# Feature-major norms: means from one full-width matmul, and roots over rows as one power instruction on GpSimd

## The chip, the cores and the metric

One core of one Trainium2 chip runs the whole kernel in one launch. The metric is the device time of an execution in microseconds: 1962.84 us, the median of 3 runs (1962.72 to 1962.88).

## The reference

One layer of a hybrid decoder, for a prompt of 1024 tokens and 8 samples of 8 tokens, 1024 features each. Two gated feed-forward blocks enclose a mixing block with two head groups side by side (sliding-window attention, and a gated linear recurrence):

```python
def rms_norm(x, g):
    xf = x.astype(jnp.float32)
    y = xf * lax.rsqrt(jnp.mean(xf * xf, axis=-1, keepdims=True) + EPS)
    return (y * g.astype(jnp.float32)).astype(x.dtype)
...
x = x + 0.5 * rms_norm(swiglu(rms_norm(x, norm_ffn1_pre[l]), ffn1_w_gu[l], ffn1_w_down[l]), norm_ffn1_post[l])
h = rms_norm(x, norm_mix_pre[l])
z = h @ w_in[l] + b_in[l]
...                                  # attention -> a, recurrence -> o
a = rms_norm(a, attn_out_norm[l])
o = rms_norm(o, hg_out_norm[l]) * jax.nn.silu(hg)
x = x + rms_norm(jnp.concatenate([a, o], axis=-1) @ w_out[l], norm_mix_post[l])
x = x + 0.5 * rms_norm(swiglu(rms_norm(x, norm_ffn2_pre[l]), ffn2_w_gu[l], ffn2_w_down[l]), norm_ffn2_post[l])
```

So there are six norms over 1024 features per token, one over 512 features of the attention output, and one over 128 features per head of the recurrence output. Each needs a mean of squares and the inverse of a square root per token.

## The kernel before

**Products.** Tokens are cut into three groups: group 0 holds 256 prompt tokens and the 64 sample tokens (320 wide), groups 1 and 2 hold 384 prompt tokens each. A large product is made of three passes over operands that are split into a rounded high part and a low rest (`mm3`, L244 to L248: high x high, high x low, low x high). A weight tile arrives by DMA in `raw` (3 buffers), ACT casts the high part and DVE subtracts for the low part (`split`, L225 to L227), both into slots of the pool `wsp` (8). Products accumulate in four PSUM banks `mm`; four more, `ax`, serve transposes, scores and the norms. SBUF scratch tiles of up to 512 columns come from the pool `t2` (8 buffers).

**Order of the work.** The first feed-forward block runs group 0 alone at first (`pre_first`, `up0`), then all groups; the mixing block runs group by group, with the mixer of a group (`attn_block`, `intra`, `hgrn_block`) as a generator that advances between the large products (`tick`, `stream`); the second feed-forward block closes. Norm work of a group is also such a generator. The final order on every engine is made by a scheduler that goes by a model of the time; some instructions are bound to come after others (`tc.issue_after`).

**Two layouts of a norm.** Where features lie on partitions (feature-major, tokens along the free axis), squares are summed over the eight chunks of features into `ss` [128, w], and the sum over partitions must come from PE. `bcast_steps` (L276) does it for the first norm of groups 1 and 2 (`pre_x`) and for the norms of group 0 (`post_t`, `pre_t`); `pre_first` (L556) does it with `roots` (L639) for the first norm of all. The steps are: a 32-bit product of each 128-token piece of `ss` with a column `omean` of 1/1024 (`st`, L297 or L643), which puts means on partitions; the root on a [128, 3] tile; three diagonal matrices (`dg`, L305 or L650); and a product of `ones` with them (`rb`, L309 or L663), which spreads each token's root over all partitions. `rb` stays in its PSUM bank until the scaling is done (`pre_first` copies it to SBUF, L664). That happens eight times in an execution.

Where tokens lie on partitions (rows), ACT sums squares along the free axis and the root is on a tile of 1, 3 or 4 columns: `row_rms` (L369), `post_n` (L399), `finish_attn` (L1186), `finish_hgrn` (L1358) and `each` (L1739), 30 roots in all. `each` runs once per 128 rows of the last result: behind the last large product of its rows it adds (L1016), squares, takes the root, scales and adds the residual (L1742), and stores.

**The root.** `rsqrt` (L201 to L218) is a bit trick and two polynomial steps on DVE, eight instructions over several columns and six over one. ACT and POOL have no part in it.

Of the kernel before, what the change touches and what calls it, by code (L numbers as in the profile page):

```python
# [8 lines left out]
F32 = mybir.dt.float32  # L9
# [9 lines left out]
P = 128  # L19
# [26 lines left out]
def tile_step(ctx: ExitStack, tc: tile.TileContext, A: dict, O: list):  # L46
# [67 lines left out]
                pass  # L114


    ident = cp.tile([P, P], F32, name="ident")
    make_identity(nc, ident)
    ones = cp.tile([P, P], F32, name="ones")
    V.memset(ones, 1.0)  # L120
    junk = cp.tile([P, 512], BF16, name="junk")
    omean = cp.tile([P, 1], F32, name="omean")
    V.memset(omean, 1.0 / D)
    S.activation(junk[:, :P], ones, AF.Silu)
    cols = cp.tile([P, NROWS], F32, name="cols")
# [75 lines left out]
    def rsqrt(y, x, wk):  # L201
# [15 lines left out]
        V.scalar_tensor_tensor(q, t, -40.0 / 3 * RS ** 6, t, op0=ALU.add, op1=ALU.mult)  # L217
        V.scalar_tensor_tensor(y, q, 80.0 * RS ** 12, y, op0=ALU.add, op1=ALU.mult)  # L218

    def small():  # L220
        return pp.tile([P, 4, 8], F32, tag="small", bufs=10, name=uid("sm"))

# [50 lines left out]
    def tmp2(name, shape=(P, 512)):  # L273
        return pp.tile(list(shape), F32, tag="t2", bufs=8, name=uid(name))

    def bcast_steps(part, w, out, add=None):  # L276

        ss = tmp2("ss")
        for d in range(KC):
            if d == 0:  # L280
                S.activation(ss[:, :w], part(d), AF.Square)
                continue
            sq = tmp2("sq")
            S.activation(sq[:, :w], part(d), AF.Square)
            (G if add else V).tensor_tensor(ss[:, :w], ss[:, :w], sq[:, :w], op=ALU.add)
            if d % 3 == 0 or add:
                yield
        yield
        nb = (w + P - 1) // P
        bank = axbank("st")  # L290
        sm = small()
        full = w // P
        if w % P:
            V.memset(sm[:, 0, 0:nb], 1.0)
        for c in range(nb):
            n = min(P, w - c * P)
            PE.matmul(bank[:n, c:c + 1], ss[:, c * P:c * P + n], omean, start=True, stop=True)  # L297
        V.tensor_scalar(sm[:, 0, 0:full], bank[:, 0:full], EPS, None, op0=ALU.add)
        if w % P:
            V.tensor_scalar(sm[:w % P, 0, full:nb], bank[:w % P, full:nb], EPS, None, op0=ALU.add)  # L300
        rsqrt(sm[:, 1, 0:nb], sm[:, 0, 0:nb], (sm[:, 2, 0:nb], sm[:, 3, 0:nb]))
        dg = tmp2("dg")
        for c in range(nb):
            n = min(P, w - c * P)
            V.tensor_scalar(dg[:, c * P:c * P + n], ident[:, :n], sm[:, 1, c:c + 1], None, op0=ALU.mult)  # L305
        yield
        yield
        rb = axbank("rb")
        PE.matmul(rb[:, :w], ones, dg[:, :w], start=True, stop=True)  # L309
        out.append(rb)  # L310
        yield

    def post_t(y, xsrc, gpost, xdst=None):

        w = WIDTH[0]

        def part(d):
            return y[d // 4][:, d % 4, :w]

        rb = []  # L320
        yield from bcast_steps(part, w, rb)
        for d in range(KC):
            xt = tmp2("xt")
            nc.sync.dma_start(xt[:, :w], xsrc(d))
            V.scalar_tensor_tensor(part(d), part(d), gpost[:, d:d + 1], rb[0][:, :w],
                                   op0=ALU.mult, op1=ALU.mult)
            G.tensor_tensor(part(d), part(d), xt[:, :w], op=ALU.add)
            if d % 2:
                yield
        if xdst is not None:  # L330
            for hf in range(2):
                nc.sync.dma_start(xdst[:, 4 * hf:4 * hf + 4], y[hf][:, :, :w])

    def pre_t(y, gpre, h):
        w = WIDTH[0]

        def part(d):
            return y[d // 4][:, d % 4, :w]

        rb = []  # L340
        yield from bcast_steps(part, w, rb)
        h[0] = new_h(0)
        for d in range(KC):
            t = tmp2("ht")
            V.scalar_tensor_tensor(t[:, :w], part(d), gpre[:, d:d + 1], rb[0][:, :w],
                                   op0=ALU.mult, op1=ALU.mult)
            hi, lo = hcol(h[0], d, w)
            split(hi, lo, t[:, :w], G)
            if d % 2:
                yield  # L350


    def row_rms(n, y, blocks, sm, dst=None):

        b0, b1 = blocks[0], blocks[-1] + 1
        if rows_of(n, b1 - 1) < P:
            V.memset(sm[:, 0, :], 1.0)
        for i in blocks:
# [10 lines left out]
        rsqrt(sm[:, 1, b0:b1], sm[:, 0, b0:b1], (sm[:, 2, b0:b1], sm[:, 3, b0:b1]))  # L369

    def gain_row(ap, scale, hf):
        g = tmp2("gb")
# [17 lines left out]
    def post_n(n, y, sm, xsrc, xdst=None):  # L390
# [8 lines left out]
        rsqrt(sm[:, 1, 0:3], sm[:, 0, 0:3], (sm[:, 2, 0:3], sm[:, 3, 0:3]))  # L399
        for i in range(3):  # L400
            if i:
                xt = load(i)
# [49 lines left out]
    def pre_x(n, y, gpre, part, SF):  # L452
# [5 lines left out]
        yield from bcast_steps(x_part, 384, rb, True)  # L458
        part[n] = y
        for d in range(KC):  # L460
            V.scalar_tensor_tensor(x_part(d), x_part(d), gpre[:, d:d + 1], rb[0][:, :384], op0=ALU.mult, op1=ALU.mult)
# [94 lines left out]
    def pre_first(x, gpre, h, raws, wts):  # L556
# [1 line left out]


        w = WIDTH[0]  # L560
        sm = small()
# [15 lines left out]

        def x_part(d):
            return x[d // 4][:, d % 4]

        V.memset(sm[:, 0, :], 1.0)

        def half(n, k, e="V"):
            raw, (hi, lo) = raws[n], tiles[n]
# [48 lines left out]
            wts.fill(2)  # L633
        second = [mmbank(), mmbank()]
        rb = tmp2("rb")[:, :w]
        dg = tmp2("dg")
        st = axbank("st")

        def roots():  # L639
            with after("PE"):  # L640
                for i in range(3):
                    r = rows_of(0, i)
                    order("PE", PE.matmul(st[:r, i:i + 1], ss[:, i * P:i * P + r], omean, start=True, stop=True))  # L643
            with after("V"):
                V.tensor_scalar(sm[:, 0, 0:2], st[:, 0:2], EPS, None, op0=ALU.add)
                V.tensor_scalar(sm[:NS, 0, 2:3], st[:NS, 2:3], EPS, None, op0=ALU.add)
                rsqrt(sm[:, 1, 0:3], sm[:, 0, 0:3], (sm[:, 2, 0:3], sm[:, 3, 0:3]))
                for i in range(3):
                    r = rows_of(0, i)
                    order("V", V.tensor_scalar(dg[:, i * P:i * P + r], ident[:, :r], sm[:, 1, i:i + 1], None,  # L650
                                               op0=ALU.mult))

        for n, bank in enumerate(second):
            wt = wts.ready.pop(0)
            for d in range(KC):
                if n == 0 and d == 4:
                    roots()
                    with after("V"):
                        wts.fill()
                if n == 1 and d == 4:  # L660
                    with after("PE"):
# [422 lines left out]
    def mixing(tp, h):  # L1084
# [96 lines left out]
        def finish_attn(n, o, r, sl):  # L1181
# [169 lines left out]
        def finish_hgrn(n, bank, r, c0):  # L1351
# [6 lines left out]
            rsqrt(sm[:r, 1, :4], sm[:r, 0, :4], (sm[:r, 2, :4], sm[:r, 3, :4]))  # L1358
# [372 lines left out]
    def each(i):  # L1731
        need("half")
        y, sm = f2.ys[2], small()
        x, t = sm[:, 0, 1:2], sm[:, 0, 2:3]
# [3 lines left out]
        V.tensor_scalar(x, sm[:, 0, 0:1], 1.0 / D, tail["sm"][:, 1, i:i + 1], op0=ALU.mult, op1=ALU.add)  # L1738
        rsqrt(sm[:, 1, 0:1], x, (t, sm[:, 0, 3:4]))  # L1739
        t0 = 384 + i * P  # L1740
        for hf, src in ((0, yg), (1, y[1][:, i])):
            V.scalar_tensor_tensor(src, src, sm[:, 1, 0:1], tail["x"][hf][:, i], op0=ALU.mult, op1=ALU.add)  # L1742
# [87 lines left out]
```

## Time and profile before

| | |
|---|---|
| time, median of 3 runs | 1962.84 us |
| the profiled execution | 1962.94 us, span 1960.9 us |
| TensorE clock granted, mean | 0.999 |
| feature-major norms in an execution | 8 |
| `st` products (L297, L643), passes on PE | 42 + 6 |
| `rb` products (L309, L663), passes on PE | 14 + 2 |
| roots by `rsqrt` (instructions on L213) | 38 |
| instructions on DVE, on POOL | 2519, 161 |

PE is TensorE, DVE is VectorE, ACT is ScalarE, POOL is GpSimd and SP is SyncE; PEld is TensorE loading weights beside its products. A row of a group of instructions names line, engine, operation and tile (out<-in), then its count, its busy time and the mean of one in ns, then the idle time of the engine just before it and what ended that. A row of the timeline gives start, duration, engine, line and tile; in brackets stands the idle time just before it. A 32-bit product is recorded as two passes (x2). Times are us from the start of the span unless ns is said.

### The profile page before, as it was taken

The numbers are of one execution on the slowest core, as the hardware profiler recorded it, in microseconds if no ns is written. First come the engines' busy times: TensorE is split into PE (matmuls) and PEld (weight loads), VectorE is DVE, ScalarE is ACT, GpSimd is POOL, SyncE is SP. The second block draws the span as 40 slices with busy tenths as digits, with TensorE's granted clock in tenths as the row PEclk, the third lists the DMA queues.
The fourth block names the chain that finished last, engine by engine and source line by source line (L and its number), as shares of the span: only waits on it lengthen the run. The fifth ranks groups of instructions, "written<-read, shape, count | busy, mean of one in ns | idle before, by whom it ended". The sixth has DMA issues, their size and how long they took to land.

```text
span 1960.9 us, 33822 instructions
## 1 busy us (share of the span) xinstructions
PE 1946.4 (99%) x13119; PEld 1821.5 (93%) x13119; DVE 1413.4 (72%) x2519; ACT 942.5 (48%) x1694; POOL 168.3 (9%) x161
## 2 busy tenths in 40 slices
PE   9999999999999999999999999999999999999998
PEld 8999999999998988778999898989999999999886
DVE  7696769886558756777677757755987877655667
ACT  5553434444445444435345545765544444444452
POOL 0400000000004102011121203000000000000201
PEclk9999999999999999999999999999999999999999
DMA  7634547555676547764434344536555645677874
GB/s 242 205 118 169 209 166 250 198 185 194 230 240 222 178 143 238 269 199 154 117 99 151 97 136 130 163 125 222 169 201 194 215 172 187 213 233 239 302 256 141
DMA packets 174161, 371.04 MB, mean 189 GB/s; under 512 B 15968, under 2 KB 66848, under 8 KB 173984
## 3 DMA queue, kind: packets, MB, share of 16 engines
q1 hardware_dynamic: 168096, 358.06, 54.8%
q10 hardware_dynamic: 5904, 10.82, 1.6%
q8 instruction: 103, 1.69, 0.3%
q14 instruction: 58, 0.48, 0.1%
HBM read 286.41 MB, written 83.39 MB: 189 GB/s over the span
## 4 chain that ended last, share of the span: by engine, by line
PE 98%; DVE 1%; ACT 0%; DMA 0%; POOL 0%; issue 0%; SPq 0%; DVEq 0%; ACTq 0%; POOLq 0%
PE mm L246 29%; PE mm L247 29%; PE mm L248 29%; PE sc L1216 1%; PE c L248 1%; PE c L246 1%; PE c L247 1%; PE pv L1255 1%; PE lv L1302 1%; PE pT L1244 1%; PE av L1389 0%; PE u L1396 0%; PE av L1392 0%; DMA big<-in_ffn_w_gu_dram 0%; PE su L1512 0%; PE tr L435 0%
## 5 line engine op out<-in xcount | busy, mean ns | idle before, releaser
L246 PE MATMUL mm<-h,wsph 128*128 128x320 f32 (+1 forms) x1296 | 412.7, 320 | 0.0
L247 PE MATMUL mm<-h,wsph 128*128 128x320 f32 (+1 forms) x1296 | 410.9, 317 | 0.0
L248 PE MATMUL mm<-h,wspl 128*128 128x320 f32 (+1 forms) x1296 | 408.4, 316 | 0.6 <-DVE wspl L227 0.6
L227 DVE TENSOR_TENSOR wspl<-raw,wsph 128x1024 fp32r<-128x1024 f32 x204 | 252.6, 1239 | 140.1 <-ACT wsph L226 135.9
L226 ACT CAST wsph<-raw 128x1024 fp32r<-128x1024 f32 x204 | 213.6, 1049 | 289.9 <-PE mm L247 229.1
L226 ACT CAST w<-raw 128x512 fp32r<-128x512 f32 (+1 forms) x212 | 156.9, 744 | 205.5 <-PE mm L247 105.3
L246 PEld LDWEIGHTS mm<-h,wsph 128*128 128x128 f32 x1296 | 243.1, 188 | 8.6 <-issue 7.1
L247 PEld LDWEIGHTS mm<-h,wsph 128*128 128x128 f32 x1296 | 243.5, 188 | 4.4 <-issue 3.4
L248 PEld LDWEIGHTS mm<-h,wspl 128*128 128x128 f32 x1296 | 243.0, 188 | 1.9 <-DVE wspl L227 0.9
L246 PE MATMUL mm<-h,w 128*128 128x384 f32 (+1 forms) x720 | 240.5, 334 | 1.1 <-ACT h L596 1.1
L247 PE MATMUL mm<-h,w 128*128 128x384 f32 (+1 forms) x720 | 240.6, 334 | 0.2 <-DVE h L598 0.2
L227 DVE TENSOR_TENSOR w<-raw,w 128x512 fp32r<-128x512 f32 (+1 forms) x212 | 179.7, 851 | 83.4 <-ACT w L226 83.0
L248 PE MATMUL mm<-h,w 128*128 128x384 f32 (+1 forms) x720 | 235.2, 334 | 0.4 <-POOL w L589 0.4
L247 PE MATMUL mm<-w,h 128*128 128x512 f32 x462 | 181.1, 392 | 0.0
L248 PE MATMUL mm<-w,h 128*128 128x512 f32 x462 | 180.3, 392 | 0.0
L246 PE MATMUL mm<-w,h 128*128 128x512 f32 x462 | 179.4, 392 | 0.0
L247 PE MATMUL mm<-big,w 128*128 128x384 f32 x528 | 176.5, 334 | 0.0
L246 PE MATMUL mm<-big,w 128*128 128x384 f32 x528 | 176.4, 334 | 0.0
L248 PE MATMUL mm<-big,w 128*128 128x384 f32 x528 | 176.1, 334 | 0.0
L246 PEld LDWEIGHTS mm<-h,w 128*128 128x128 f32 x720 | 135.2, 188 | 1.4 <-ACT h L596 1.3
L247 PEld LDWEIGHTS mm<-h,w 128*128 128x128 f32 x720 | 135.2, 188 | 0.4 <-DVE h L598 0.4
L248 PEld LDWEIGHTS mm<-h,w 128*128 128x128 f32 x720 | 134.7, 188 | 0.7 <-POOL w L589 0.7
(346 smaller groups left out, 3454.9 us busy)
## 6 DMA issues: line engine op xcount, KB each, us to landing
raw<-in_ffn_w_gu_dram SPq DMA_DIRECT2D x158, 512.0 KB
raw<-in_ffn_w_down_dram SPq DMA_DIRECT2D x74, 512.0 KB
raw<-in_w_in_dram SPq DMA_DIRECT2D x54, 512.0 KB
ar<-fa SPq DMA_DIRECT2D x70, 384.0 KB
big<-in_ffn_w_down_dram SPq DMA_DIRECT2D x88, 256.0 KB
fb<-big SPq DMA_DIRECT2D x44, 512.0 KB
fa<-big SPq DMA_DIRECT2D x22, 768.0 KB
raw<-fb SPq DMA_DIRECT2D x30, 512.0 KB
```

What stands on the lines that cost most here:

```text
L226: made['S'] = S.copy(hi, src).ins
L227: (lo_eng or V).tensor_tensor(lo, src, hi.bitcast(F32), op=ALU.subtract)
L246: PE.matmul(out, a[0], b[0], start=first, stop=False, skip_group_check=resume)
L247: PE.matmul(out, a[0], b[1], start=False, stop=False, skip_group_check=resume)
L248: return PE.matmul(out, a[1], b[0], start=False, stop=last, skip_group_check=resume).ins
L1216: PE.matmul(banks[g][:, i * 256:i * 256 + wk], zq[64 * g:64 * g + 64, 2 * pr + i, b * P:(b + 1) * P], kx[64 * g:64 * g + 64, k0:k0 + wk], ...
L1244: PE.transpose(bank[:, (kb * 2 + i) * P:(kb * 2 + i + 1) * P], pt[g][:, i, kb * P:(kb + 1) * P], ident)
L1255: PE.matmul(ob[64 * g:64 * g + 64, pr * 256:pr * 256 + 256], vn[:, vb, 64 * g:64 * g + 64], pT[g][:, kb * 256:kb * 256 + 256], start=kb == ...
L1302: PE.matmul(b5[32 * i:32 * i + 32, b, a], K[:, a, cs], Q[:, a, cs], start=True, stop=True)
```

## The change

Feature-major: `omean` becomes a [128, 128] matrix of 1/1024, so that one 32-bit product of it with `ss` leaves every token's mean on all partitions. The root is then taken by `rsqrt` over the whole width in SBUF, and its result `rb` is used from there. The three `st` products, the diagonals and the product of `ones` with them go, as does the copy in `pre_first`. In `pre_first`, product and root are issued where `roots` stood, and no later instruction is bound to come after the last step of the root.

Rows: `root` is one power instruction on POOL with a constant tile of -0.5 as second operand, in all five places.

```diff
+    mhalf = cp.tile([P, 8], F32, name="mhalf")
+    V.memset(mhalf, -0.5)
-    omean = cp.tile([P, 1], F32, name="omean")
+    omean = cp.tile([P, P], F32, name="omean")
     V.memset(omean, 1.0 / D)
...
+    def root(y, x):
+        G.tensor_tensor(y, x, mhalf[:y.shape[0], :y.shape[-1]], op=ALU.pow)
...
+    def mean_root(rb, ss, order=None):
+        w = rb.shape[-1]
+        bank = axbank("rb")
+        PE_ = PE.matmul(bank[:, :w], omean, ss, start=True, stop=True)
+        x, t = tmp2("mx")[:, :w], tmp2("mt")[:, :w]
+        V.tensor_scalar(x, bank[:, :w], EPS, None, op0=ALU.add)
+        rsqrt(rb, x, (t, x))
+        return PE_
...
     def bcast_steps(part, w, out, add=None):
...
-        for c in range(nb):
-            n = min(P, w - c * P)
-            PE.matmul(bank[:n, c:c + 1], ss[:, c * P:c * P + n], omean, start=True, stop=True)
...
-        rsqrt(sm[:, 1, 0:nb], sm[:, 0, 0:nb], (sm[:, 2, 0:nb], sm[:, 3, 0:nb]))
-        dg = tmp2("dg")
-        for c in range(nb):
-            n = min(P, w - c * P)
-            V.tensor_scalar(dg[:, c * P:c * P + n], ident[:, :n], sm[:, 1, c:c + 1], None, op0=ALU.mult)
+        rb = tmp2("rb")[:, :w]
+        mean_root(rb, ss[:, :w])
         yield
         yield
-        rb = axbank("rb")
-        PE.matmul(rb[:, :w], ones, dg[:, :w], start=True, stop=True)
         out.append(rb)
...
     # pre_first
                 if n == 0 and d == 4:
-                    roots()
-                    with after("V"):
-                        wts.fill()
-                if n == 1 and d == 4:
-                    with after("PE"):
-                        rbank = axbank("rb")
-                        order("PE", PE.matmul(rbank[:, :w], ones, dg[:, :w], start=True, stop=True))
-                    S.copy(rb, rbank[:, :w])
+                    with after("PE"), after("V"):
+                        order("PE", mean_root(rb, ss[:, :w]))
+                    wts.fill()
...
     # finish_attn; in row_rms, post_n, finish_hgrn and each in the same way
-            rsqrt(sm[:r, 1, 0:1], sm[:r, 0, 0:1], (sm[:r, 2, 0:1], sm[:r, 3, 0:1]))
+            root(sm[:r, 1, 0:1], sm[:r, 0, 0:1])
```

More of the change, by code (lines that the diff above doesn't have):

```diff
@@ L288, in bcast_steps @@
         yield
[L289 to L294, printed above, removed]
-        for c in range(nb):
-            n = min(P, w - c * P)
[L297 to L300, printed above, removed]
-        rsqrt(sm[:, 1, 0:nb], sm[:, 0, 0:nb], (sm[:, 2, 0:nb], sm[:, 3, 0:nb]))
-        dg = tmp2("dg")
-        for c in range(nb):
-            n = min(P, w - c * P)
-            V.tensor_scalar(dg[:, c * P:c * P + n], ident[:, :n], sm[:, 1, c:c + 1], None, op0=ALU.mult)
+        rb = tmp2("rb")[:, :w]
+        mean_root(rb, ss[:, :w])
         yield
         yield
-        rb = axbank("rb")
-        PE.matmul(rb[:, :w], ones, dg[:, :w], start=True, stop=True)
         out.append(rb)
@@ L324, in post_t @@
             nc.sync.dma_start(xt[:, :w], xsrc(d))
-            V.scalar_tensor_tensor(part(d), part(d), gpost[:, d:d + 1], rb[0][:, :w],
+            V.scalar_tensor_tensor(part(d), part(d), gpost[:, d:d + 1], rb[0],
                                    op0=ALU.mult, op1=ALU.mult)
@@ L344, in pre_t @@
             t = tmp2("ht")
-            V.scalar_tensor_tensor(t[:, :w], part(d), gpre[:, d:d + 1], rb[0][:, :w],
+            V.scalar_tensor_tensor(t[:, :w], part(d), gpre[:, d:d + 1], rb[0],
                                    op0=ALU.mult, op1=ALU.mult)
@@ L368, in row_rms @@
                                op0=ALU.add, op1=ALU.add)
-        rsqrt(sm[:, 1, b0:b1], sm[:, 0, b0:b1], (sm[:, 2, b0:b1], sm[:, 3, b0:b1]))
+        root(sm[:, 1, b0:b1], sm[:, 0, b0:b1])
     def gain_row(ap, scale, hf):
@@ L398, in post_n @@
         V.scalar_tensor_tensor(sm[:, 0, 0:3], sm[:, 0, 0:3], EPS, sm[:, 0, 4:7], op0=ALU.add, op1=ALU.add)
-        rsqrt(sm[:, 1, 0:3], sm[:, 0, 0:3], (sm[:, 2, 0:3], sm[:, 3, 0:3]))
+        root(sm[:, 1, 0:3], sm[:, 0, 0:3])
         for i in range(3):
@@ L460, in pre_x @@
         for d in range(KC):
-            V.scalar_tensor_tensor(x_part(d), x_part(d), gpre[:, d:d + 1], rb[0][:, :384], op0=ALU.mult, op1=ALU.mult)
+            V.scalar_tensor_tensor(x_part(d), x_part(d), gpre[:, d:d + 1], rb[0], op0=ALU.mult, op1=ALU.mult)
             if d % 2:
@@ L560, in pre_first @@
         w = WIDTH[0]
-        sm = small()
         spare = axbank()
@@ L579, in x_part @@
             return x[d // 4][:, d % 4]
-        V.memset(sm[:, 0, :], 1.0)
         def half(n, k, e="V"):
@@ L635, in pre_first @@
         rb = tmp2("rb")[:, :w]
-        dg = tmp2("dg")
-        st = axbank("st")
-        def roots():
-            with after("PE"):
-                for i in range(3):
-                    r = rows_of(0, i)
-                    order("PE", PE.matmul(st[:r, i:i + 1], ss[:, i * P:i * P + r], omean, start=True, stop=True))
-            with after("V"):
[L645 to L651, printed above, removed]
         for n, bank in enumerate(second):
@@ L656, in pre_first @@
                 if n == 0 and d == 4:
-                    roots()
-                    with after("V"):
-                        wts.fill()
-                if n == 1 and d == 4:
-                    with after("PE"):
-                        rbank = axbank("rb")
-                        order("PE", PE.matmul(rbank[:, :w], ones, dg[:, :w], start=True, stop=True))
-                    S.copy(rb, rbank[:, :w])
+                    with after("PE"), after("V"):
+                        order("PE", mean_root(rb, ss[:, :w]))
+                    wts.fill()
                 with after("PE"):
@@ L1357, in finish_hgrn @@
             V.tensor_scalar(sm[:r, 0, :4], sm[:r, 0, :4], 1.0 / P, EPS, op0=ALU.mult, op1=ALU.add)
-            rsqrt(sm[:r, 1, :4], sm[:r, 0, :4], (sm[:r, 2, :4], sm[:r, 3, :4]))
+            root(sm[:r, 1, :4], sm[:r, 0, :4])
             V.tensor_tensor(o[:r], b4[:r], sm[:r, 1, :4].unsqueeze(2).to_broadcast([r, 4, P]), op=ALU.mult)
@@ L1733, in each @@
         y, sm = f2.ys[2], small()
-        x, t = sm[:, 0, 1:2], sm[:, 0, 2:3]
+        x = sm[:, 0, 1:2]
         S.activation(junk, y[0][:, i], AF.Square, accum_out=sm[:, 0, 0:1])
@@ L1738, in each @@
         V.tensor_scalar(x, sm[:, 0, 0:1], 1.0 / D, tail["sm"][:, 1, i:i + 1], op0=ALU.mult, op1=ALU.add)
-        rsqrt(sm[:, 1, 0:1], x, (t, sm[:, 0, 3:4]))
+        root(sm[:, 1, 0:1], x)
         t0 = 384 + i * P
```

## Prediction

> **What bounds the kernel now.** I read the busy times first, then the stages, then who waits for whom. The page of the kernel before, its first part and the shares of its chain:
>
> ```profile
> PE 1946.4 (99%) x13119; PEld 1821.5 (93%) x13119; DVE 1413.4 (72%) x2519; ACT 942.5 (48%) x1694; POOL 168.3 (9%) x161
> PE 98%; DVE 1%; ACT 0%; DMA 0%; POOL 0%; issue 0%; SPq 0%; DVEq 0%; ACTq 0%; POOLq 0%
> ```
>
> The reader sees one engine carrying everything: TensorE (PE) is busy for 1946.4 of 1960.9 us, and the chain that ended last is PE for 98%. A busy PE need not be PE at its best, so the stages matter (stretch, length, then PE, PEld, DVE, ACT and POOL busy):
>
> ```profile
> 10.00:20.00 10.00, 8.89 (x60) 8.34 (x59) 9.53 (x23) 7.85 (x16) 1.48 (x1) 1.00 0.75 280
> 60.00:100.00 40.00, 38.97 (x265) 38.17 (x264) 30.69 (x60) 20.99 (x33) 12.61 (x9) 1.00 0.52 169
> 960.00:1330.00 370.00, 367.83 (x3468) 332.17 (x3467) 260.16 (x559) 200.96 (x413) 56.09 (x48) 1.00 0.41 129
> 1950.00:1961.00 11.00, 3.46 (x16) 2.52 (x14) 6.93 (x21) 0.97 (x4) 0.00 (x0) 0.84 0.26 100
> ```
>
> The other stretches that I asked for between 20 and 1950 us are full to the hundredth. So PE idles at the start, about 1 us in 60 to 100, 2.2 us in the mixing stage, and 7.5 us after its last matmul. Three waits of PE on other engines touch the change:
>
> ```profile
> PE av L1392 <- DVE big L1341: 1.4, 1, 1.4
> PE st L297 <- POOL ss L285: 1.0, 1, 1.0
> PE st L643 <- DVE ss L625: 0.5, 1, 0.5
> ```
>
> Two kinds of edit count, then: those that change PE's own stream, and those in the last 7.5 us. Everything else on DVE or POOL is hidden as long as PE keeps its supply.
>
> **Part 1, the means: PE loses 24 matmuls.** Each of eight feature-major norms now runs three products of the summed squares with a column (`st`), a root on a [128, 3] tile, three diagonals `dg`, and a product of `ones` with them (`rb`). The change keeps one product of the shape of `rb` and drops `st`. Three of the eight places, first, second and last, in the order of time (start, us, engine, line):
>
> ```profile
> 18.57 0.81 PE L643 MATMUL st<-omean,ss 128*128 128x1 f32 x6 [0.48 <-DVE ss L625]
> 19.31 0.42 PE L246 MATMUL mm<-h,wsph 128*128 128x320 f32 x1
> 19.57 0.31 PE L247 MATMUL mm<-h,wsph 128*128 128x320 f32 x1
> ...
> 62.48 0.31 PE L248 MATMUL mm<-h,wspl 128*128 128x320 f32 x1
> 62.63 0.72 PE L297 MATMUL st<-omean,ss 128*128 128x1 f32 x6
> 63.22 0.39 PE L246 MATMUL mm<-h,wsph 128*128 128x320 f32 x1
> 63.45 0.31 PE L247 MATMUL mm<-h,wsph 128*128 128x320 f32 x1
> ...
> 1802.81 0.39 PE L248 MATMUL mm<-w,h 128*128 128x512 f32 x1
> 1803.04 0.70 PE L297 MATMUL st<-omean,ss 128*128 128x1 f32 x6
> 1803.67 0.50 PE L246 MATMUL mm<-w,h 128*128 128x512 f32 x1
> 1804.01 0.39 PE L247 MATMUL mm<-w,h 128*128 128x512 f32 x1
> ```
>
> The price of a group is read from starts: from its own start to that of the second matmul behind it, less one ordinary step. At 62.63 it is 63.45 - 62.63 - 0.15 = 0.67 us (62.63 - 62.48 is the ordinary step); at 1803.04 it is 0.97 - 0.23 = 0.74; at 18.57 it is 1.00 - 0.15 = 0.85. The other five lie between 0.64 and 0.77 by the same reading. Sum of eight: **-5.9 us**, all on the engine that is the chain.
>
> The product that stays costs what it cost:
>
> ```profile
> 585.67 0.70 PE L309 MATMUL rb<-dg,ones 128*128 128x320 f32 x2
> 585.97 0.64 PE L247 MATMUL mm<-w,h 128*128 128x512 f32 x1
> 586.45 0.40 PE L248 MATMUL mm<-w,h 128*128 128x512 f32 x1
> ```
>
> From 585.67 to 586.45 less a step is 0.55 us. Its operands change places (`omean` is stationary, `ss` moves) but the sizes are the same, so I cost the exchange at nothing. It now stands where `st` stood and takes over that wait for `ss`.
>
> Against this: the built order of the changed kernel has 313 changes between the 32-bit products and the split ones on PE, against 315 before, although dropping eight groups should take away 12 to 16. So five to seven small groups more stand alone among the large products. The row at 1803.67 shows what a return costs: 0.34 us to the next start and not 0.23, so 0.11. I add **+0.6 us** (0 to +0.8).
>
> **Part 2, the wide root on DVE.** A root over [128, 320 or 384] is nine passes over the width, in place of the small ones and the diagonals. The rows of the first norm now, and of a pass of that width:
>
> ```profile
> 19.57 0.15 DVE L645 TENSOR_SCALAR sm<-st 128x2 f32<-128x2 f32 x1
> 22.02 2.35 DVE L227 TENSOR_TENSOR wspl<-raw,wsph 128x1024 fp32r<-128x1024 f32 x2
> 25.83 0.48 DVE L742 TENSOR_TENSOR sg<-mm,rb 128x320 f32<-128x320 f32 x1
> 26.23 0.48 DVE L744 TENSOR_TENSOR su<-mm,rb 128x320 f32<-128x320 f32 x1
> ```
>
> and the cast to the high half that goes ahead of a weight subtraction (count, busy, mean ns):
>
> ```profile
> L226 ACT CAST wsph<-raw 128x1024 fp32r<-128x1024 f32 x204 | 213.6, 1049 | 289.9 <-PE mm L247 229.1
> ```
>
> Now the chain is 22.02 - 19.57 = 2.45 us; nine passes at 0.40 (26.23 - 25.83) are 3.6. DVE thus gains about 1.2 us of work in each of eight norms, some 9 us in all, and loses far more in part 3. Hidden from 60 us on, since DVE is 72% busy and PE never waits for these roots today. At the start DVE is full, so there I followed the order of the built program: the nine passes stand among weight subtractions (1.18 us each) that used to come later, and the last subtraction ahead of the first user of `rb` needs a weight slot that PE has still to free. From 19.1 us PE has half a unit of 24 matmuls left and then whole ones at 24 x 0.147 = 3.5 us: 20.9, 24.4, 27.9, 31.5. The slot comes free at 27.9, cast (1.05) and subtraction end at about 30.2, and the first user starts there, against 25.83 now. PE wants the bank that it frees at 31.5, and the parts of `h` behind it with margins of 0.2 to 1.2 us by the same count. I take **+0.3 us** (0 to +1.0). `rb` now holds an SBUF buffer of eight instead of a PSUM bank of four through the scaling; the order already contains that.
>
> **Part 3, 30 roots over rows on POOL.** Each drops six to eight DVE instructions and adds a trip to POOL and back. Only the last of them is on the path, behind PE's last matmul:
>
> ```profile
> 1953.49 0.69 DVE L1016 TENSOR_TENSOR big<-mm,big 128x512 f32<-128x512 f32 x1 [0.27 <-PE mm L248]
> ...
> 1955.03 0.21 DVE L1738 TENSOR_SCALAR sm<-sm,sm 128x1 f32<-128x1 f32 x1
> 1955.28 0.15 DVE L213 TENSOR_SCALAR sm<-sm 128x1 int32<-128x1 int32 x1
> ...
> 1956.37 0.16 DVE L218 SCALAR_TENSOR_TENSOR sm<-sm 128x1 f32<-128x1 f32 x1
> 1956.56 0.75 DVE L1742 SCALAR_TENSOR_TENSOR yg<-yg,sm,big 128x512 f32<-128x512 f32 x1
> ```
>
> That is 1956.56 - 1955.28 = 1.28 us gone. No power operation is in this trace; the nearest small ones on POOL are these:
>
> ```profile
> L1288 POOL TENSOR_TENSOR big<-big 128x8 f32<-128x8 f32 x1 | 0.2, 201 | 0.1
> L1288 POOL TENSOR_TENSOR big<-big 128x64 f32<-128x64 f32 x1 | 1.4, 1355 | 0.1
> ```
>
> Bounds: 0.2 us from below, and 1.4 from above, a row far above its neighbours. I take 0.5 for the power, since it is nearest to the 8-wide product and more work, and 0.3 for the two hops: **-0.5 us** (-0.9 to +0.4). POOL is empty from 1950 us on, so nothing is queued ahead.
>
> The other 29 lie beside PE. In the built order, DVE's reader stands directly behind its writer for 12 of the 30, so DVE is held there for the whole trip, about 0.8 us where it used to work about 1.28. POOL's long multiplications of the same layer end before the first root of the layer's blocks is due, so I expect no queue. What is behind a held DVE is the next weight subtraction; its cover is the lead that this row shows, in which DVE idles for ACT:
>
> ```profile
> 1239.56 1.22 DVE L227 TENSOR_TENSOR wspl<-raw,wsph 128x1024 fp32r<-128x1024 f32 x1 [3.14 <-ACT wsph L226]
> ```
>
> I cost these at nothing (-2 to +2 us: today's PE waits gone, or as many new).
>
> **The sum.** -5.9 + 0.6 + 0.3 - 0.5 = -5.5 us against the profiled execution's 1962.94: 1957.4. The median of the runs is 0.10 lower: **1957.3 us**.
>
> **Rivals.**
> - *New waits on DVE and POOL eat the gain* (0.14). For it: the order of the whole mixing stage is shuffled, and the margins at the start are below 1 us. Against: a held DVE comes out ahead of today's 1.28 us. With all ends at their worst, 0.8 + 1.0 + 0.4 + 2 - 5.9 = -1.7: about 1961.
> - *A slow power* (0.08), the slower side. [...] If one root takes r us, the tail pays about twice (r - 1.1), since the second block's chain ends only just ahead of 1953.49, and each of the 12 holds pays what exceeds 1.1 + 3.1. Gain and bound together are 5.5 + 3.9 = 9.4; it decides from r of about 4.4 us, and at r = 5 gives 2 x 3.9 + 12 x 0.8 - 5.0 = +12: 1975. Against: no small row of POOL is over 1.4 us.
> - *One long first root* (0.06), if POOL has to fetch the power's code. One POOL instruction of this trace did last far beyond its kind (min/median/max ns):
>
> ```profile
> L285 POOL TENSOR_TENSOR ss<-ss,sq x14: 1012/1019/5107, 51.9 to 75.7; 128x384 f32<-128x384 f32 x14
> ```
>
>   A first root of 5.1 us plus 0.3 for the hops, less a lead of 3.1, brings 2.3 us to PE in the mixing stage: about 1959.6. Against: POOL's first product of two tensors took no longer than its second.
>
> ```profile
> 7.98 1.28 POOL L589 TENSOR_TENSOR w<-big,w 128x512 fp32r<-128x512 f32 x1 [5.68 <-ACT w L587]
> 11.28 1.48 POOL L589 TENSOR_TENSOR w<-big,w 128x512 fp32r<-128x512 f32 x1 [2.02 <-ACT w L587]
> ```
>
>   [...]
> - *The 24 matmuls are no gain* (0.06): PE only waits elsewhere for the weights' DMA, and the time stays near 1962.5. Against: PE has no DMA wait from 20 us on.
>
> **How the numbers follow.** Forecast 0.66, all of it below 1958.9, which is 0.2% (3.9 us) under the median and about what a measurement of this kernel can tell from no change. The first, third and fourth rivals end within 0.2%: 0.26. The slow power is slower: 0.08. The range goes from -8.8, the best ends of all parts (-5.9 - 0.9 - 2), to -1.7, the worst ones: 1954.0 to 1961.2; outside lie the slow power, the fourth rival and little else.
>
> **What would show it.** PE's matmuls fall by 48 passes (13119 counts two of each) and its busy time by some 6 us. L297 and L643 are gone, and one two-pass group stands at each of eight places. From the last row pass of the tail to the first product with the residual: under 1.28 us. POOL gains 30 short instructions; their length decides between forecast and slow power. PE waits naming POOL `sm` or DVE in the mixing stage, over 2 us in sum, would make the prediction wrong; so would a wait for `h` between 31 and 46 us.

## The result, and the profile after

The changed kernel takes **1969.14 us**, the median of 8 runs (1966.31 to 1970.13), against 1962.87 of before in the same series (1962.72 to 1963.33): a ratio of 1.003, with a 95% interval of 1.0021 to 1.004. It is slower by 6.3 us; 5.5 us faster was forecast. The profiled execution took 1968.62 us with a span of 1966.9.

The page of the kernel after, busy times and the shares of the chain:

```profile
PE 1948.6 (99%) x13071; PEld 1817.6 (92%) x13071; DVE 1409.2 (72%) x2268; ACT 940.9 (48%) x1693; POOL 203.6 (10%) x191
...
PE 91%; DVE 2%; DMA 1%; issue 1%; ACT 1%; SPq 0%; DVEq 0%; POOLq 0%; POOL 0%; ACTq 0%
```

The 48 passes on PE are gone (13119 to 13071), DVE has 251 instructions fewer and POOL 30 more, as the edit says. But PE's busy time rose by 2.2 us where 6 less was forecast, and the chain is PE for 91% only: other engines now hold PE up. Stretches of the kernel after (length, then PE, PEld, DVE, ACT, POOL busy):

```profile
60.00:100.00 40.00, 39.05 (x261) 38.25 (x261) 37.45 (x49) 22.08 (x33) 13.13 (x9) 1.00 0.61 204
960.00:1330.00 370.00, 366.53 (x3434) 327.96 (x3433) 248.73 (x447) 197.46 (x411) 71.81 (x62) 1.00 0.40 126
```

Between 60 and 100 us DVE went from 30.69 to 37.45 us, though it has fewer instructions there (49 for 60): they got longer. PE's waits in the kernel after (us in total, times, longest):

```profile
PE mm L252 <- DVE w L232: 2.3, 2, 1.4
PE av L1364 <- DVE big L1313: 1.4, 1, 1.4
PE pT L1216 <- ACT t L1205: 1.3, 2, 1.2
...
PE mm L251 <- DVE big L993: 0.7, 1, 0.7
...
PE mm L252 <- DVE h L232: 0.7, 1, 0.7
```

All but the second are new, and none names POOL `sm`, the wait that I had feared most. The sign that I had set for a wrong prediction, new waits of PE for DVE or POOL `sm` in the mixing stage, did not show: there the only wait of PE for DVE is the old one of 1.4 us.

**Where the time went.** Both kernels run the same 10242 split products. By their names and shapes in the traces, some 390 stand at another place in the order after the change, all of them between 20 and 50, 110 and 160, 590 and 630, and 840 and 870 us; the others keep their place, and nearly the same holds for the experiments. So the start of the n-th one in each kernel shows how far it is ahead (-) or behind, in us against before:

| at (us of before) | after | rows alone | means alone, root in PSUM | whole change, both repairs |
|---|---|---|---|---|
| 30 | -1.40 | -0.52 | -1.42 | -0.95 |
| 60 | -0.01 | -0.52 | -0.67 | 0.09 |
| 100 | -1.42 | -0.54 | -2.06 | -2.53 |
| 560 | -1.22 | -0.54 | -2.06 | -2.52 |
| 700 | 0.91 | -0.54 | -3.58 | -4.04 |
| 1200 | -1.25 | -1.78 | 0.06 | -6.38 |
| 1330 | 6.27 | 5.76 | 0.05 | -7.82 |
| 1790 | 6.29 | 5.75 | 0.04 | -7.80 |
| 1850 to the end | 6.66 | 5.75 | -0.72 | -8.56 |

(The last three columns are experiments, below.) Two things must be kept in mind. Each column starts with a lead of 0.5 to 0.66 us that it has from the first 10 us, before any product of the change runs: in the kernel before, PE's first large product waited 1.1 us for ACT and started later than in the others. And the row at 1200 us catches a moment: in the kernel after, two groups of small products, 1.9 us in all, stand four split products later, while at 1190 and 1230 us its column reads 0.7. So the column of after has three places of loss: 1.4 us in 30 to 60, 2.1 in 560 to 700, and 5.5 in 1230 to 1330. The first and second lie beside feature-major norms, the third in the mixing stage, where roots over rows stand. Behind the last product the new kernel gains 0.6 us.

**The second place, read from the trace.** DVE of the kernel after from 583 us on, and PE's product that waits for it:

```profile
583.94 7.53 DVE L322 SCALAR_TENSOR_TENSOR big<-big,halfpost,rb 128x320 f32<-128x320 f32 x8
591.38 1.89 DVE L232 TENSOR_TENSOR w<-raw,w 128x1024 fp32r<-128x1024 f32 x1
```

```profile
593.32 0.50 PE L252 MATMUL mm<-w,h 128*128 128x512 f32 x1 [1.43 <-DVE w L232]
```

Eight scalings take 7.53 us, the weight subtraction behind them ends at 593.27, and PE has stood since 591.9. POOL's additions run beside them:

```profile
584.63 9.38 POOL L324 TENSOR_TENSOR big<-big,xt 128x320 f32<-128x320 f32 x8 [357.80 <-DMA xt<-in_x0T_dram]
```

Here are the same scalings by their line, before and then after (min/median/max ns):

```profile
L325 DVE SCALAR_TENSOR_TENSOR big<-big,halfpost,rb x16: 542/543/548, 586.4 to 1816.2; 128x320 f32<-128x320 f32 x16
```

```profile
L322 DVE SCALAR_TENSOR_TENSOR big<-big,halfpost,rb x16: 539/1160/1169, 583.9 to 1823.7; 128x320 f32<-128x320 f32 x16
L322 DVE SCALAR_TENSOR_TENSOR big<-big,cols,rb x8: 546/547/548, 1030.5 to 1033.8; 128x320 f32<-128x320 f32 x8
```

Same shape, same count, 543 ns then 1160. What changed is where `rb` lies: a PSUM bank before, SBUF now. And the second row of after is the same instruction at 547 ns, from 1030.5 to 1034.3 us, where POOL's additions (L324) start only at 1034.6. **Theory A**: with both tensors in SBUF the scaling and POOL's addition beside it slow each other, and the weights queued behind reach PE late. **Theory B**: the rest is the roots over rows, whose trip to POOL holds DVE and so the mixing stage. The **rival** to both is that neither matters by itself: the scheduler wrote another order for PE's small products.

### The profile page after: what moved, and what is told of

Read it like the earlier page. It is cut to its first block, busy times and chain, and to the rows that moved or that the text cites. A ratio compares the mean times of both kernels' runs of the same rounds, so it can differ in the third digit from the quotient of the medians.

```text
span 1966.9 us, 33517 instructions
## 1 busy us (share of the span) xinstructions
PE 1948.6 (99%) x13071; PEld 1817.6 (92%) x13071; DVE 1409.2 (72%) x2268; ACT 940.9 (48%) x1693; POOL 203.6 (10%) x191
## 4 chain that ended last, share of the span: by engine, by line
PE 91%; DVE 2%; DMA 1%; issue 1%; ACT 1%; SPq 0%; DVEq 0%; POOLq 0%; POOL 0%; ACTq 0%
PE mm L251 27%; PE mm L252 27%; PE mm L253 27%; DMA ar<-fa 1%; PE sc L1188 1%; PE pv L1227 1%; PE c L253 1%; PE c L251 1%; PE c L252 1%; PE pT L1216 1%; PE lv L1274 1%; DVE big L322 1%; PE av L1361 0%; DVE w L232 0%; PE u L1368 0%
## 5 line engine op out<-in xcount | busy, mean ns | idle before, releaser
L232 DVE TENSOR_TENSOR wspl<-raw,wsph 128x1024 fp32r<-128x1024 f32 x204 | 257.3, 1263 | 134.0 <-ACT wsph L231 132.5
```

The source lines that it names most:

```text
L232: (lo_eng or V).tensor_tensor(lo, src, hi.bitcast(F32), op=ALU.subtract)
```

## The experiments

Each was timed in five rounds beside the kernel before, which took 1962.68 to 1962.72 us in these series.

**1. Four kernels that take the change apart.** The means alone:

```diff
     # the changed kernel, in all five places
-            root(sm[:r, 1, 0:1], sm[:r, 0, 0:1])
+            rsqrt(sm[:r, 1, 0:1], sm[:r, 0, 0:1], (sm[:r, 2, 0:1], sm[:r, 3, 0:1]))
```

> Only the feature-major part: the means by one product, the wide root on DVE, rb in an SBUF buffer; every root over rows stays the Newton chain on DVE. Theory A (two SBUF inputs of the scalings run beside POOL's additions and slow each other; PE waits about 4.6 us for the weights queued behind them) and theory B (the roots over rows on POOL cost some 6.7 us net in the mixing stage) together: -5.9 +0.6 +4.6 +0.9 (start) = about 1963.1, the scalings with halfpost at about 1.16 us each. Rival to both (all of the loss is from the roots over rows): about 1957.5, the scalings harmless to PE.

The roots over rows alone (the five calls of `root` put into the kernel before):

> Only the roots over rows as one power on POOL; the means, diagonals and the PSUM bank of rb as before the change. Theory B: +7.3 us of PE's waits and single groups between 860 and 1330 us, less 0.6 in the tail: about 1969.5. If theory A carries the whole loss: about 1962.3.

The whole change with `rb` in PSUM again, and the means alone with it (the very first norm, in `pre_first`, keeps its root in SBUF in both):

```diff
-    def rsqrt(y, x, wk):
+    def rsqrt(y, x, wk, out=None):
...
-        V.scalar_tensor_tensor(y, q, 80.0 * RS ** 12, y, op0=ALU.add, op1=ALU.mult)
+        V.scalar_tensor_tensor(y if out is None else out, q, 80.0 * RS ** 12, y, op0=ALU.add, op1=ALU.mult)
...
-        rsqrt(rb, x, (t, x))
+        rsqrt(rb, x, (t, x), bank[:, :w] if psum else None)
...
     # bcast_steps
-        rb = tmp2("rb")[:, :w]
-        mean_root(rb, ss[:, :w])
+        rb = mean_root(tmp2("my")[:, :w], ss[:, :w], True)
```

> The changed kernel with the last step of the wide root written into the PSUM bank of the mean, so that the scalings again have one SBUF input and one PSUM input. Theory A: the scalings with halfpost go back from 1.16 to 0.54 us beside the same POOL additions, PE's waits at 591, 617, 642 and 1825 us go, about 4.6 us less than the changed kernel: 1964.5. Rival (the slow scalings are hidden, or POOL alone slows them): 1969, and 1.16 us stays if POOL alone does it.

> Only the feature-major part, with the root written into the PSUM bank; the roots over rows on DVE. Theories A and B together: -5.9 +0.6 +0.9 = about 1958.5, the fastest of the four. If the loss comes from the new order of PE's work and not from A or B: within 1 us of the kernel with the means alone.

| | us | ratio to before, 95% |
|---|---|---|
| means alone | 1965.67 | 1.0012 (1.0003 to 1.0021) |
| rows alone | 1968.22 | 1.0026 (1.0015 to 1.0036) |
| whole change, root in PSUM | 1965.32 | 1.0013 (1.0004 to 1.0022) |
| means alone, root in PSUM | 1961.92 | 0.9999 (0.999 to 1.0008) |

**Theory A holds.** The medians put the bank at 3.8 us in both pairs (1969.14 to 1965.32, 1965.67 to 1961.92). The times of the last kernel scatter widely (1959.98 to 1967.71), and its interval overlaps that of the means alone, so the second pair is weak by itself. The traces are not: between 560 and 700 us after and the means alone lose 2.1 and 1.5 us against before, and both kernels with the bank gain 1.5. The scalings of the whole change with the root in PSUM, beside the same additions on POOL:

```profile
L321 DVE SCALAR_TENSOR_TENSOR big<-big,halfpost,rb x16: 542/542/548, 583.4 to 1818.5; 128x320 f32<-128x320 f32 x16
584.05 9.27 POOL L323 TENSOR_TENSOR big<-big,xt 128x320 f32<-128x320 f32 x8 [357.80 <-DMA xt<-in_x0T_dram]
```

POOL's additions differ as well, if less clearly: the median of all 24 is 1123 ns in the kernel after and 882 here, while the eight from 584 us on take 9.38 and 9.27 us in sum.

The medians of the scaling side by side: 1160 ns with both tensors in SBUF and additions beside (kernel after), 547 with both in SBUF and no addition beside (kernel after, the row with `cols`), 542 with `rb` in PSUM and additions beside.

Theory B's number came near (1969.5 expected, 1968.22 measured). But the means alone came 2.6 us above the 1963.1 expected, and the last kernel missed by 3.4 us, with no root on POOL in it at all: it lost 3.6 us between 700 and 1200 where the two norms in that stretch should have won 1.5. Of the 5 us, 1.6 belong to the profiled execution, in which PE's granted clock (third column from the end) fell for a moment:

```profile
840.00:850.00 10.00, 10.00 (x63) 8.76 (x62) 8.57 (x17) 4.79 (x11) 0.60 (x1) 0.86 0.74 234
```

The other 3.5 strike a mixing stage that has no root on POOL.

**A third theory.** The longer steps of PE at 1245 us, where "rows alone" and after lose 1.6 us at once, lead to it. PE's small products there in the kernel before:

```profile
1245.79 1.08 PE L1255 MATMUL pv<-t,vn 128*64 128x256 f32 x8
1246.80 1.13 PE L1216 MATMUL sc<-kx,big 64*128 64x256 f32 x8
1247.87 0.49 PE L1389 MATMUL av<-big,big 128*128 128x128 f32 x2
```

and in the kernel after:

```profile
1243.75 0.65 PE L1227 MATMUL pv<-t,vn 128*64 128x256 f32 x2
1244.33 1.13 PE L1188 MATMUL sc<-kx,big 64*128 64x256 f32 x4
1245.38 1.08 PE L1227 MATMUL pv<-t,vn 128*64 128x256 f32 x6
1246.39 1.13 PE L1188 MATMUL sc<-kx,big 64*128 64x256 f32 x4
1247.45 0.49 PE L1361 MATMUL av<-big,big 128*128 128x128 f32 x2
```

The reader sees the same 8 + 8 passes take 2.08 us before and 3.70 after. Eight scores in one go cost 1.07 us (1246.80 to 1247.87), and four cost 1.06. The shapes and the starts say why: `sc` uses 64 rows of the array and `pv` 64 columns, one half for each of two heads, and the program gives the heads in turn. Standing next to each other two heads run side by side: in a whole group the trace has the passes start in pairs, 6 to 7 ns apart. Where the scheduler puts something between them, each half runs alone: the four scores at 1244.33 start one by one, 215 ns and more apart.

**Theory C**: the loss in the mixing stage is split pairs. PE's time for `sc`, and then for `pv`, in the whole execution (first column after the length), of before:

```profile
0.00:1970.00 1970.00, 21.36 (x128) 12.91 (x128) 22.45 (x64) 1.00 0.57 188
0.00:1970.00 1970.00, 19.04 (x120) 7.90 (x120) 4.68 (x8) 1.00 0.57 188
```

of after, and "rows alone" has the same two PE values:

```profile
0.00:1970.00 1970.00, 23.86 (x128) 14.12 (x128) 22.53 (x64) 1.00 0.56 188
0.00:1970.00 1970.00, 21.59 (x120) 8.61 (x120) 4.70 (x8) 1.00 0.56 188
```

40.40 us became 45.45. (These busy times count the overlap of a product's end with the next one. Counted from start to next start, as the expectations below do, it is 38.4 and 42.9: 4.55 us more.) The scheduler's order has 12 whole groups of scores and 10 of `pv` before, 9 and 6 after. The means alone with the root in PSUM fit too: with no root on POOL that kernel has 10 and 9 whole groups and 42.86 us of busy time, 2.5 more than before, of the 3.5 that were left open.

**2. Pairs bound together.** In `attn_block` each of these products is bound to come after the one ahead of it, heads in turn, the second head first because its operand is ready later:

```diff
-                    for g in range(2):
-                        PE.matmul(banks[g][:, i * 256:i * 256 + wk], ...
+                    for g in (1, 0):
+                        with tc.issue_after(prev) if prev else nullcontext():
+                            prev = PE.matmul(banks[g][:, i * 256:i * 256 + wk], ...).ins
...                  # and the same for the products into ob
```

> The kernel before the change, with the products of each attention block bound to follow one another on PE (two heads alternate, the second head first, the four scores behind the four value products): theory C says that two heads' half-array products run side by side when they stand next to each other, so that a whole group costs 1.0 us and a split one 1.6 to 2.1. Scores and value products together now take 38.4 us; with 13 whole groups of each and 3 split ones some 34.8: 3.5 us less, about 1959.3. Rival (the pairs do not matter, the mixing stage waits on DVE, ACT or POOL): 1962.7, unchanged.

> The roots over rows on POOL as the only part of the change, with the attention products bound in the same way. Theory C: the loss of this part is the split pairs, 42.9 us of scores and value products against 34.8 when bound, so 1968.2 - 8.1 = about 1960, within 1 us of the bound kernel before. Theory B (the loss is the trip to POOL and back with DVE held behind it): the two bound kernels still differ by about 5.5 us, 1965 here.

> The whole change with the attention products bound. Theory C: 1969.1 - 8.1 = about 1961; what is left above the forecast is theory A's 3.7 us. Theory B: about 1967.

> The version that the theories point to: means by one product with the root written into the PSUM bank, the power on POOL only for the last rows (each), every other root over rows on DVE, attention products bound. From the kernel with the means and the bank: -5.3 for the pairs, -0.6 for the tail: 1961.9 - 5.9 = about 1956. If pairs do not matter: 1961.3.

| | us | `sc` + `pv` us, unbound to bound | ratio to before, 95% |
|---|---|---|---|
| before, bound | 1960.13 | 40.40 to 37.14 | 0.9989 (0.998 to 0.9998) |
| rows alone, bound | 1958.29 | 45.45 to 36.50 | 0.9975 (0.9965 to 0.9985) |
| whole change, bound | 1959.04 | 45.45 to 36.50 | 0.9979 (0.997 to 0.9988) |
| means in PSUM, power in the tail, bound | 1956.59 | (no unbound twin) 37.83 | 0.9973 (0.9964 to 0.9983) |

The place shown above, in "rows alone, bound":

```profile
1241.69 1.08 PE L1262 MATMUL pv<-t,vn 128*64 128x256 f32 x8
1242.71 1.13 PE L1222 MATMUL sc<-kx,big 64*128 64x256 f32 x8
1243.77 0.49 PE L1397 MATMUL av<-big,big 128*128 128x128 f32 x2
```

and its `sc` and `pv`:

```profile
0.00:1970.00 1970.00, 19.38 (x128) 11.53 (x128) 22.17 (x64) 1.00 0.57 188
0.00:1970.00 1970.00, 17.12 (x120) 7.38 (x120) 4.69 (x8) 1.00 0.57 188
```

**Theory C holds and theory B falls.** Binding takes 9.9 us from "rows alone" (1968.22 to 1958.29) and 10.1 from the whole change, for 8.95 us less of these products (8.2 by starts); PE's wait of 1.3 us for `pT` is gone with it. The expectations (1959.3, 1960, 1961 and 1956 in the order of the table) were met within 2 us; the times of the last one fall into two groups, six low and five high (see the last section). Bound against bound, the roots over rows on POOL are 1.8 us *faster* than on DVE (1960.13 to 1958.29), with all 30 trips in place; "within 1 us" was expected. The two intervals overlap, but the 11 and 8 times themselves hardly do (1959.66 and up, 1959.72 and down). That the scheduler's model of the power and of DVE's shorter chains is what shuffles the order is only argued; what is shown is the order and its price.

**3. Both repairs, the start, the additions and the tail.**

> The whole change with both repairs: the root written into the PSUM bank and the attention products bound. Theory A adds to theory C: 1959.0 - 3.7 = about 1955.3. If the slow scalings were only late because the mixing stage was late: 1959.

The next kernel is the same, with `roots` and the copy of the kernel before put back into `pre_first`:

> As the kernel with both repairs, but the first norm of all taken the old way (columns, diagonals, copy to SBUF). The start alone decides: the new first norm saves 0.6 to 0.9 us by 20 us and 0.5 more by 30, and loses it again to waits for parts of h by 60 us, so the two differ by under 0.5 us. If the start's loss is a real cost of the wide root, this kernel is 1 us or more faster.

The next is the changed kernel with one edit:

```diff
-            G.tensor_tensor(part(d), part(d), xt[:, :w], op=ALU.add)
+            V.tensor_tensor(part(d), part(d), xt[:, :w], op=ALU.add)
```

> The changed kernel with the additions behind the scalings of group 0 moved from POOL to DVE; rb stays in SBUF. Theory A: with no addition on POOL beside them, the scalings with halfpost take 0.55 us each in place of 1.16, though both inputs are still in SBUF; but DVE then adds 0.48 to 0.55 us for each addition itself, so the weights behind them come as late as before and the time stays near 1968.5. Rival (two SBUF inputs with a column operand are slow by themselves there): 1.16 stays and the time grows by some 4 us.

The last is the kernel before with `root` in `each` alone:

> The kernel before the change with the power on POOL in each alone, three roots. The built order of PE is that of before (12 whole score groups, 10 whole value groups). Tail alone: 1962.7 - 0.6 = 1962.1. If any instruction on POOL disturbs PE's supply: above 1963.

| | us | ratio to before, 95% |
|---|---|---|
| whole change, both repairs | 1953.96 | 0.996 (0.9949 to 0.9971) |
| the same, first norm as before | 1952.98 | 0.995 (0.9938 to 0.9962) |
| changed kernel, additions on DVE | 1965.96 | 1.0017 (1.0008 to 1.0025) |
| power in the tail alone | 1962.12 | 0.9996 (0.9988 to 1.0005) |

The repairs add up, to 1.3 us more than expected (1955.3): with the pairs bound the bank brings 5.1 us (1959.04 to 1953.96), not 3.8. In the unbound kernels it had parted more pairs: `sc` and `pv` took 46.57 us there against 45.45, and 42.86 against 41.73 with the means alone. The second kernel is the fastest, about 10 us ahead of before and 16 ahead of the change as made. Its lead over the first, 1.0 us, lies at my bound of 1 us for "a real cost", and the intervals of the two overlap: that the wide first root costs anything is not settled, but no gain of it shows either. In the two profiled executions the first kernel loses 0.3 us between 17 and 60 us and the second none. (The 0.6 to 0.9 us "by 20 us" of the expectation was mostly the lead of every kernel over before, not the norm's.)

With the additions on DVE the scalings came back to 548 ns with both inputs in SBUF, as theory A wants:

```profile
L322 DVE SCALAR_TENSOR_TENSOR big<-big,halfpost,rb x16: 546/548/552, 584.0 to 1822.6; 128x320 f32<-128x320 f32 x16
```

Its time is a miss: 1968.5 expected, 1965.96 measured. In its trace the wait at 591 us is gone too, because the scheduler now puts the weight subtractions among the additions on DVE (at 588.15, where after has 591.38); between 560 and 640 us it gains 1.5 us, as the kernels with the bank do. What the additions cost DVE comes later in this execution, the slowest of its eleven (1968.84), as a wait of PE:

```profile
641.62 0.61 PE L251 MATMUL mm<-h,wsph 128*128 128x320 f32 x1 [2.24 <-DVE big L988]
```

Whether the faster executions have that wait is not known. The tail alone came as expected (1962.1), with the two PE values of `sc` and `pv` as in before: 1962.68 to 1962.12, an effect inside its interval, but see the rows of the tail below.

## Why the prediction was wrong

**What held.** *Eight groups of `st` gone, -5.9 us.* In the kernel with the means alone and the root in PSUM, the six norms outside the mixing stage show it without disturbance: 0.77 for the first (from -0.65 at 17 us to -1.42 at 24), 1.39 for two between 60 and 100, 1.52 for two between 560 and 700, 0.76 at 1800. That is 0.70 to 0.77 each, against 0.64 to 0.85. The two inside the mixing stage can't be told apart from the rest there. The product that stays, in the kernel after:

```profile
17.91 0.81 PE L284 MATMUL rb<-ss,omean 128*128 128x320 f32 x2 [0.48 <-DVE ss L619]
18.32 0.55 PE L251 MATMUL mm<-h,wsph 128*128 128x320 f32 x1
18.70 0.31 PE L252 MATMUL mm<-h,wsph 128*128 128x320 f32 x1
```

From 17.91 to 18.70 less a step of 0.15 it costs 0.64 (0.55 was read at 585 us), and it took over the wait for `ss`, as said.

*The tail, -0.5 us.* The kernel after, behind its last product:

```profile
1961.69 0.21 DVE L1710 TENSOR_SCALAR sm<-sm,sm 128x1 f32<-128x1 f32 x1
1961.99 0.55 POOL L223 TENSOR_TENSOR sm<-sm,mhalf 128x1 f32<-128x1 f32 x1 [4.20 <-DVE sm L1710]
1962.57 0.75 DVE L1714 SCALAR_TENSOR_TENSOR yg<-yg,sm,big 128x512 f32<-128x512 f32 x1 [0.66 <-POOL sm L223]
```

The wait of 0.66 us stands where 1.28 us of root stood: -0.6. Power 0.55 and hops 0.11 (0.66 - 0.55), against 0.5 and 0.3. The 0.3 was my estimate, with no row behind it.

*Slow power, long first root, no gain from the matmuls.* None of the three came. The longest power took 2.05 us, far from the 4.4 at which that rival decides, and the first one 0.57.

**What failed.**

1. *"`rb` now holds an SBUF buffer of eight instead of a PSUM bank of four through the scaling; the order already contains that"* (part 2, costed at nothing). This was the step with the largest error of thought: I asked only whether a buffer is free, not what an instruction costs that reads it: a scaling went from 543 to 1160 ns. It cost **+3.8 us** (two pairs of kernels; 5.1 with the pairs bound). The nine passes at 0.40 that I did cost were hidden from 60 us on, as said.

2. *"The other 29 roots ... I cost these at nothing (-2 to +2 us)"* (part 3). By themselves, bound against bound, rows are worth -1.8 us with the tail, so about -1.2 without it, inside my bounds. But the same edit rewrote the order of the mixing stage, and that cost **+5.05 us** of `sc` and `pv` (40.40 to 45.45; 4.55 by starts). What I looked at was not the price: DVE held at POOL was to be it, and no product of PE waited for POOL `sm`.

3. *"313 changes against 315 ... I add +0.6"* (part 1). The right view, counted wrongly. I counted how often PE changes between large and small products and priced a change at 0.11. The price hangs on *which* small products are parted: a pair of halves parted costs some 0.5 us (1.06 for four alone against 1.07 for eight, for two pairs). The order that I had in hand showed whole groups falling from 12 to 9 and from 10 to 6. Nor did the extra changes belong to the means: in the traces the means alone have 297 changes (299 with the bank), 16 to 18 fewer than before, where dropping `st` was to take 12 to 16; rows alone have 329, 14 more.

4. *The start, +0.3 (0 to +1.0).* It lost 1.4 us between 30 and 60 (-1.40 to -0.01 in the table): the wait for `h` that the last part named as the sign of error came, 0.65 us at 43.6 us. Some 0.6 of the loss goes with the first step above: the whole change with the root in PSUM loses 0.8 there.

One more wait came with the new order. PE and ACT of the kernel after:

```profile
1295.03 1.13 PE L1188 MATMUL sc<-kx,big 64*128 64x256 f32 x6
...
1297.10 0.70 PE L1188 MATMUL sc<-kx,big 64*128 64x256 f32 x2
```

```profile
1299.39 1.28 ACT L690 ACT_TABLE_LOAD   x1
1300.69 0.47 ACT L690 ACTIVATE sg<-sg 128x320 f32<-128x320 f32 x1
1301.17 1.28 ACT L1205 ACT_TABLE_LOAD   x1
1302.47 0.51 ACT L1205 ACTIVATE t<-t,sm 128x256 f32<-128x256 f32 x1
```

```profile
1303.12 0.33 PE L1216 MATMUL pT<-ident,t 128*128 128x128 f32 x1 [1.18 <-ACT t L1205]
```

The last scores of this block stand behind value products, two table loads stand ahead of the exponentials, and PE asks for the transposes (`pT`) too early: 1.3 us in two waits. In "rows alone, bound" no such wait is left.

**The account.** Forecast -5.5; root in SBUF 3.8, pairs 5.05, start 1.1 more than costed, transposes behind ACT 1.3: +5.75, against +6.3 measured. The items are not independent (the bank moved pairs and part of the start, and by starts the pairs are 4.55), so the sum says that the causes are of the right size, not that the account closes to half a microsecond. With the pairs bound on both sides and the root in PSUM, the change is worth 1953.96 - 1960.13 = -6.2 us, close to the -5.5 that its parts were costed at. That is partly luck: the means and the wide root come to -4.3 (1958.29 to 1953.96; -5.0 was costed), the rows to -1.8 (-0.5 was costed). The rival "new waits eat the gain" had the right kind of place, but at 1961 it was bounded by waits that I could name.

## What to carry to other kernels

Where a result moves between PSUM and SBUF, ask for every reader how many of its inputs are then in SBUF, and what POOL runs beside it at that moment (here a scaling went from 543 to 1160 ns with POOL's additions beside it). Where a scheduler writes the order, any edit that changes durations or engines can rewrite a stage that it doesn't touch: look in the built order at the groups whose price hangs on their neighbours (here the scores of two heads: eight took 1.07 us next to each other, and four alone 1.06), and bind those explicitly before judging the edit.

## What the runs showed of the hardware

The power on POOL took longer with more columns. The means by form are 594 ns for one column, 1012 for three and 1288 for four (kernel after). Some of them took far longer than the rest, up to 2.05 us, and why is open; the shortest of each took 548, 849 and 1009 ns, which is about 0.15 us per column on top of a fixed 0.4:

```profile
L223 POOL TENSOR_TENSOR sm<-sm,mhalf 128x4 f32<-128x4 f32 x8 | 10.3, 1288 | 36.2 <-DVE sm L1329 36.1
L223 POOL TENSOR_TENSOR sm<-sm,mhalf 128x3 f32<-128x3 f32 x9 | 9.1, 1012 | 149.3 <-DVE sm L395 119.3 <-DVE sm L364 27.1 <-DVE sm L1415 3.0
L223 POOL TENSOR_TENSOR sm<-sm,mhalf 128x1 f32<-128x1 f32 x11 | 6.5, 594 | 140.3 <-DVE sm L1157 126.1 <-DVE sm L1710 14.2
```

In two kernels a pause of PE was followed by a lower granted clock. In "means in PSUM, power in the tail, bound", whose eleven times fall into two groups (1955.2 to 1956.6 and 1960.3 to 1961.6), the profiled run is of the later group. PE waits 2.06 us for a DVE product that took 2.38 us, with a POOL product of 2.45 us beside it (the four of this kind took 0.67 to 0.68 us in the kernel before), and then its steps are 0.32 us where 0.17 was usual, at a granted clock of 0.73 in the next stretch:

```profile
888.78 2.26 PE L1486 MATMUL su<-t,t 32*128 32x512 f32 x4 [2.06 <-DVE t L1471]
...
891.46 0.52 PE L252 MATMUL mm<-h,wsph 128*128 128x384 f32 x1
891.78 0.52 PE L253 MATMUL mm<-h,wspl 128*128 128x384 f32 x1
```

```profile
880.00:890.00 10.00, 7.60 (x66) 5.64 (x66) 6.46 (x10) 3.77 (x7) 3.12 (x2) 0.93 0.81 239
890.00:900.00 10.00, 10.00 (x50) 8.71 (x47) 8.99 (x37) 5.32 (x18) 0.92 (x1) 0.73 0.61 185
```

The wait of 2.24 us at 641.62 in the kernel with the additions on DVE was followed by a lower clock too: 0.83 granted from 640 to 650 us, and 1.00 in each of the next five stretches of 10 us. The pauses of 1.4 us in the kernel after were not followed by this: its clock was 1.00 in every stretch of 10 us up to the tail. Slower steps also came without a pause. In "means alone, root in PSUM" the steps went from 0.23 to 0.43 us between 839.9 and 842.5 (the row at 840 us, above), with PE busy all through the ten microseconds before. What sets them off there is open, whether the pause did so in the other two was not tested, and neither was whether it makes the two groups of times.
